# Seven block products instead of eight in eight chunks of each up-projection, on one Trainium2 core

## The chip, the cores and the metric

The kernel runs on one core of one Trainium2 chip. The metric is the device time of one execution in microseconds, 1455.82 us in the median of three runs before the change (1455.78 to 1455.86). The engines of the core are TensorE (PE in the profile, its weight loads PEld), VectorE (DVE), ScalarE (ACT), GpSimd (POOL) and SyncE (SP); all work in their own order and wait for each other on semaphores. SP and POOL issue the transfers here.

## The reference, cut to what matters

Two layers on a sequence of 512 tokens with 1024 features: attention and a gated FFN, then a recurrent block and a gated FFN. What the change touches is the first half of the FFN:

```python
def conv_ffn(x, w_up, conv_w, conv_b, w_down):
    u = causal_dwconv(x @ w_up, conv_w, conv_b)      # w_up: 1024 x 6144, conv over 3 tokens
    g, v = u[..., :D_FF], u[..., D_FF:]              # D_FF = 3072
    return (jax.nn.gelu(g, approximate=True) * v) @ w_down
```

All is float32.

## The kernel before

**Precision.** Each float32 operand is split into two float32r tiles, a rounded one (hi) and the rest (lo). `split` (line 148) is an ACT copy for hi and a DVE subtraction for lo. A product is three matmuls, hi by hi, hi by lo and lo by hi (`PASSES`, `mm3`, line 257).

**The up-projection.** Features lie on partitions and tokens in the free dimension. A weight chunk is 256 columns of w_up, a load of 1 MB that SP issues (`load`, line 193). It makes two units of 128 columns, hi and lo. A tile is one unit against the transposed activations hT: 8 blocks of 128 features, three passes, 24 matmuls with 512 tokens each, into one PSUM bank (`feat`). For each of 12 values of j, `ffn` (line 591) runs four tiles: two Gelu tiles (chunk j of the g half) and two value tiles (chunk j of the v half). Only the first j is made in token halves, as matmuls 256 tokens wide. After each tile `sink` (line 607) evacuates it: `conv` (line 594) is an ACT pass with scale and bias (L596) and two DVE multiply-adds that read the bank shifted by one and two tokens (L600); a Gelu tile gets an ACT Gelu (L611), a value tile a DVE product with the Gelu tile (L615). The 24 product tiles stay in SBUF for the down-projection (`rows_run`).

**What sets the order.** The schedule is written by hand: the order in the code is the order on each engine. After each tile `tick` (line 222) advances pending side work (norms) and calls `pump` (line 167), which splits the next weight units as long as fewer than 8 (`W_UNITS`) are live, and issues loads into three raw buffers. `take` (line 209) returns a unit, `done` (line 216) frees it. So weights are split up to 8 tiles ahead, and a split waits on ACT until PE has left its buffer.

**Other buffers.** The residual x lies in `x_sb`, written in `postnorm` (L411) and read in `prenorm`. The general pool `gen` has 32 tiles of 128x512, the norm gains have two tiles of 128x1024, and PSUM has 8 banks in rotation.

Of the kernel before, what the change touches and what calls it, by code (L numbers as in the profile page):

```python
# [18 lines left out]
P = 128  # L19
# [13 lines left out]
W_UNITS = 8  # L33
# [4 lines left out]
WARM = 5  # L38

# [35 lines left out]
def kernel(  # L75
# [30 lines left out]
    wp = ctx.enter_context(tc.tile_pool(name="wp", bufs=W_UNITS))  # L106
# [24 lines left out]
    x_sb = cp.tile([P, 4, D], F32, tag="x_sb", name="x_sb")  # L131
# [21 lines left out]
    state = {"dma": 0, "cv": 0, "live": 0, "next": 0, "hold": False}  # L153
# [12 lines left out]

    def pump(limit=2):

        for _ in range(limit):
            i = state["cv"]  # L170
            if not pieces and i < state["dma"]:
                pieces.extend((i, j, u) for j, u in enumerate(parts_of(plan[i][0], raws.pop(i))))
                state["cv"] += 1
            if pieces and state["live"] < W_UNITS:
                i, j, raw = pieces.pop(0)
                hi, lo = (
                    wp.tile([P] + list(raw.shape[1:]), F32R, tag=t, name=nm("w" + t)) for t in ("hi", "lo")
                )
                h = raw.shape[1] // 2
                cuts = [(slice(None), slice(0, h)), (slice(None), slice(h, 2 * h))]  # L180
                if raw.shape[1] == 1:
                    cuts = [(slice(None), slice(0, 1), slice(n, n + 512)) for n in (0, 512)]
                if plan[i][4] is not None:
                    split_normed(hi, lo, raw, plan[i][4] + (2 * j if plan[i][0] == "value" else 0))
                    cuts = []
                for c in cuts:
                    split(hi[c], lo[c], raw[c])
                units[i, j] = (hi, lo)
                state["live"] += 1
            while not pieces and state["dma"] < len(plan) and state["dma"] - state["cv"] < RAW_BUFS:  # L190
                load()
# [17 lines left out]
    def take(i, j):  # L209
        while (i, j) not in units:  # L210
            before = state["live"]
            pump(1)
            assert before != state["live"]
        return units[i, j]

    def done(n=1):
        state["live"] -= n
# [19 lines left out]
    def w_cols(w, c0, normed=False):  # L237
# [4 lines left out]
        plan.append(("feat", KD, 256, srcs, 0 if normed else None))  # L242
# [72 lines left out]
    def prenorm(t, hT, g, wait):  # L315
        xh, gh = halves(x_sb[:, t, :]), halves(g)
# [31 lines left out]
    def first_transposed(t, i):  # L348

        ps = psum("tr")  # L350
        for k in range(4 * i, 4 * i + 4):
            nc.tensor.transpose(
                ps[:, k % 4 * P : (k % 4 + 1) * P],
                x_sb[:, t, i * 512 : i * 512 + 512].rearrange("t (p k) -> t k p", k=4)[:, k % 4], ident,
            )
# [16 lines left out]
    def first_squares(i):  # L372
        for t in range(4):
            junk = gen(s="junk")
            nc.scalar.activation(
                junk, x_sb[:, t, i * 512 : i * 512 + 512], AF.Square, accum_out=first_ss[i][:, t : t + 1]
# [23 lines left out]
    def postnorm(t, banks, g, final):  # L400
# [8 lines left out]
        for i, c in enumerate(at):  # L409
            xc = x_sb[:, t, c]  # L410
# [12 lines left out]
    def feat(W, hT, dst, n0, n1):  # L423
        for k in range(KD):
            mm3(
                dst[:, n0:n1],
                [w[:, k, :] for w in W],
# [5 lines left out]
    def feat_tiles(n, hT, sink, halves=False):  # L433
# [15 lines left out]
        for c in range(n):  # L449
            i = chunk()  # L450
            for m in range(2):
                ps = psum()
                feat(take(i, m), hT, ps, 0, S)
                done()
                sink(2 * c + m, ps)
                tick()
# [18 lines left out]
    def rows_run(nchunks, A, prep, seq, order, post, pre, eng):  # L475
# [7 lines left out]
        def product(t, i, k, cols, start, stop):  # L483
            w = take(*W[k // 2][k % 2])
            c0 = i * 512
# [3 lines left out]
                [v[:, 0, c0 + cols.start : c0 + cols.stop] for v in w],  # L489
# [101 lines left out]
    def ffn(layer, hT, post, pre):  # L591
# [14 lines left out]

        def sink(b, ps, j):
            m = b % 2
            if b < 2:
                u = conv(ps, 2 * j + m)  # L610
                nc.scalar.activation(u, u, AF.Gelu_apprx_tanh)  # L611
                gv.append(u)
            else:
                u = conv(ps, 24 + 2 * j + m)
                nc.vector.tensor_tensor(gv[2 * j + m], gv[2 * j + m], u, op=ALU.mult)  # L615
# [4 lines left out]
        for j in range(12):  # L620
            if j == 11:
                prep(3)
            feat_tiles(2, hT, lambda b, ps: sink(b, ps, j), j == 0)
        return run()


    def attention(hT, post, pre):
# [50 lines left out]
        def first_values(vs):  # L678
# [4 lines left out]
            def product(t, u, which=range(6)):  # L683
                W = take(ids[u // 2], u % 2)
                steps = [(k, a, b) for a, b in PASSES for k in (2 * u, 2 * u + 1)]
                for n in which:
# [4 lines left out]
                        W[b][:, k % 2, :],  # L691
# [24 lines left out]
            done(2)  # L716
# [12 lines left out]
            done(2)  # L729
# [15 lines left out]
        def values(vs, permute, midway=None):  # L745
# [6 lines left out]
            for t in range(4):  # L752
                banks[t] = psum("v")
                for u in range(4):
                    W = take(ids[u // 2], u % 2)
                    steps = [(k, a, b) for k in (2 * u, 2 * u + 1) for a, b in PASSES]
                    for k, a, b in steps:
# [3 lines left out]
                            W[b][:, k % 2, :],  # L761
# [3 lines left out]
                    if t == 3 and u % 2:  # L765
                        done(2)
# [190 lines left out]
    def lru(hT, post, pre):  # L957
# [19 lines left out]
        def gates(n):  # L977
            W = take(chunk(), 0)
            sg = {}
            for m in range(2):  # L980
                for gx in range(2):
                    ps = psum("gate")
                    for k in range(2):
                        mm3(ps, [w[:, 2 * gx + k, m * P : (m + 1) * P] for w in W], xs[2 * n + k], k == 0, k == 1)
# [79 lines left out]
    for layer in range(2):  # L1064
# [9 lines left out]
        for j in range(12):  # L1074
            w_cols(ffn_w_up[layer], j * 256)
            w_cols(ffn_w_up[layer], D_FF + j * 256)
# [12 lines left out]
    def x_half(t, i):  # L1089
        c = slice(i * 512, (i + 1) * 512)  # L1090
        nc.sync.dma_start(x_sb[:, t, c], x[0, t * P : (t + 1) * P, c])
# [72 lines left out]
```

## Time and profile before

| What | before |
|---|---|
| median of 3 runs | 1455.82 us |
| span of the profiled execution, first to last instruction | 1454.0 us |
| what lies around the span, against the median | 1.8 us |
| mean granted TensorE clock | 0.999 |
| VectorE (DVE) busy | 879.8 us, 61% |
| ScalarE (ACT) busy | 675.9 us, 46% |
| GpSimd (POOL) busy | 133.9 us, 9% |
| moved by DMA | 172.76 MB, mean 119 GB/s |

The profile is of one execution. Its span leaves out what comes before the first and after the last instruction; the execution's own time isn't printed beside it, so 1.8 us, the median less the span, stands for that. A matmul's row is longer than the time by which the next follows it, since matmuls are pipelined; the spacing of the start times is what a matmul costs. The stretch of the chunks that change (j = 3 to 10) runs from 568.3 to 742.4 us in the first layer and from 1121 to 1295 us in the second.

### The profile page before, as it was taken

To read this page: it belongs to the slowest core of one execution; us is meant where nothing else is said; L and a number is where in the kernel's file an instruction comes from. 1 tells how busy PE (TensorE), PEld (TensorE's weight loads), DVE (VectorE), ACT (ScalarE), POOL (GpSimd) and SP (SyncE) were. 2 spreads that over 40 slices of the span, in tenths; PEclk is the share of its full clock that TensorE was granted. 3 is DMA by queue.
4 is the path that set the end of the run, shared out by engine and by line. 5 is a ranking of instruction groups with operands and counts; after the bars stand their busy time and mean duration, and the time that the engine had idled before them with its cause. 6 is when DMAs were issued, how large, how long until landed. Compare 5 with 4: busy or idle time off the path is not lost.

```text
span 1454.0 us, 18793 instructions
## 1 busy us (share of the span) xinstructions
PE 1445.0 (99%) x6861; PEld 1214.4 (84%) x6861; DVE 879.8 (61%) x1955; ACT 675.9 (46%) x1532; POOL 133.9 (9%) x275
## 2 busy tenths in 40 slices
PE   9999999999999999999999999999999999999998
PEld 7888888888888898888888888888898888888886
DVE  6767747474735975555564338769775555564333
ACT  7656636262615553343444335589453434444221
POOL 0340414040402100000000001000100000000000
PEclk9999999999999999999999999999999999999999
DMA  7653637372726343323323322432333233223201
GB/s 225 207 146 109 174 113 208 104 215 97 216 96 211 102 131 100 103 87 102 101 88 116 115 73 88 131 116 84 120 102 116 87 102 102 87 104 128 88 0 58
DMA packets 125364, 172.76 MB, mean 119 GB/s; under 512 B 8736, under 2 KB 102392, under 8 KB 125272
## 3 DMA queue, kind: packets, MB, share of 16 engines
q1 hardware_dynamic: 114280, 145.48, 31.0%
q0 software_dynamic: 10144, 25.04, 5.9%
q8 instruction: 54, 0.88, 0.2%
q10 hardware_dynamic: 848, 1.05, 0.2%
q14 instruction: 38, 0.31, 0.1%
HBM read 156.24 MB, written 15.29 MB: 118 GB/s over the span
## 4 chain that ended last, share of the span: by engine, by line
PE 93%; ACT 4%; DVE 3%; issue 1%; DVEq 0%; ACTq 0%
PE ps L259 55%; PE acc L259 24%; PE v L758 8%; PE v L688 1%; DVE xb L967 1%; PE O L909 1%; PE S L854 1%; PE S L808 1%; DVE wlo L150 1%; ACT sig L988 1%; ACT whi L149 1%; PE O L259 1%; PE tr L341 1%; ACT sig L1007 0%; ACT a L1005 0%
## 5 line engine op out<-in xcount | busy, mean ns | idle before, releaser
L259 PE MATMUL ps<-hT,whi 128*128 128x512 f32 (+1 forms) x2752 | 801.3, 375 | 0.0
L259 PEld LDWEIGHTS ps<-hT,whi 128*128 128x128 f32 x2752 | 503.6, 188 | 91.6
L259 PE MATMUL ps<-hT,wlo 128*128 128x512 f32 (+1 forms) x1376 | 515.3, 374 | 0.0
L150 DVE TENSOR_TENSOR wlo<-raw,whi 128x512 fp32r<-128x512 f32 x360 | 230.8, 686 | 187.2 <-ACT whi L149 187.1
L259 PEld LDWEIGHTS ps<-hT,wlo 128*128 128x128 f32 x1376 | 259.1, 188 | 46.5
L149 ACT ACTIVATE whi<-raw 128x512 fp32r<-128x512 f32 x360 | 204.6, 621 | 135.4 <-PE acc L259 121.0
L600 DVE SCALAR_TENSOR_TENSOR u<-ps,cols,u 128x511 f32<-128x511 f32 x192 | 143.8, 749 | 140.6 <-ACT u L596 137.2
L259 PE MATMUL acc<-whi,ahi 128*128 128x512 f32 x512 | 199.7, 390 | 0.0
L259 PE MATMUL acc<-whi,alo 128*128 128x512 f32 x512 | 199.4, 389 | 0.1
L259 PE MATMUL acc<-wlo,ahi 128*128 128x512 f32 x512 | 199.3, 389 | 0.0
L143 ACT ACTIVATE whi<-raw,first_w 128x128 fp32r<-128x128 f32 (+1 forms) x432 | 146.2, 425 | 56.6 <-PE ps L259 33.9
L596 ACT ACTIVATE u<-ps,cols 128x512 f32<-128x512 f32 x96 | 74.8, 779 | 210.0 <-PE ps L259 210.0
L144 DVE SCALAR_TENSOR_TENSOR wlo<-raw,first_w,whi 128x128 fp32r<-128x128 f32 (+1 forms) x432 | 139.5, 389 | 1.4 <-ACT whi L143 1.3
L259 PEld LDWEIGHTS acc<-whi,alo 128*128 128x128 f32 x512 | 96.1, 188 | 20.5 <-DVE alo L150 0.5
L259 PEld LDWEIGHTS acc<-whi,ahi 128*128 128x128 f32 x512 | 96.1, 188 | 19.8
L259 PEld LDWEIGHTS acc<-wlo,ahi 128*128 128x128 f32 x512 | 96.2, 188 | 19.8
L758 PE MATMUL v<-whi,hT 128*128 128x512 f32 x320 | 102.4, 393 | 0.0
L302 POOL DMA_DIRECT2D turned<-T x36 | 19.6, 547 | 763.4 <-DVE T L296 759.9
L309 POOL DMA_DIRECT2D ft<-turned x144 | 78.7, 554 | 39.6 <-issue 17.7
L758 PEld LDWEIGHTS v<-whi,hT 128*128 128x128 f32 x320 | 60.1, 188 | 12.3
L611 ACT ACTIVATE u<-u 128x512 f32<-128x512 f32 x48 | 30.3, 632 | 80.4 <-DVE u L600 80.4
L758 PE MATMUL v<-wlo,hT 128*128 128x512 f32 x160 | 62.3, 389 | 0.0
(171 smaller groups left out, 1010.7 us busy)
## 6 DMA issues: line engine op xcount, KB each, us to landing
raw<-in_ffn_w_up_dram SPq DMA_DIRECT2D x48, 1024.0 KB
raw<-in_attn_w_qkv_dram SPq DMA_DIRECT2D x67, 512.0 KB
raw<-in_ffn_w_down_dram SPq DMA_DIRECT2D x24, 1024.0 KB
raw<-in_lru_w_in_dram SPq DMA_DIRECT2D x8, 1024.0 KB
turned<-T POOLq DMA_DIRECT2D x28, 256.0 KB, 2.6
ft<-turned POOLq DMA_DIRECT2D x112, 64.0 KB, 5.8
vrows<-v SPq DMA_DIRECT2D x16, 256.0 KB
vp<-vrows SPq DMA_DIRECT2D x16, 256.0 KB
```

Source lines behind the costliest of these rows:

```text
L143: nc.scalar.activation(hi[:, k], raw[:, k], AF.Copy, scale=w)
L144: nc.vector.scalar_tensor_tensor(lo[:, k], raw[:, k], w, hi[:, k].bitcast(F32), op0=ALU.mult, op1=ALU.subtract)
L149: nc.scalar.activation(hi, raw, AF.Copy)
L150: nc.vector.tensor_tensor(lo, raw, hi.bitcast(F32), op=ALU.subtract)
L259: mm(dst, l[a], r[b], start=start and n == 0, stop=stop and n == 2)
L302: nc.gpsimd.dma_start(d, T)
L309: nc.gpsimd.dma_start(t[32 * c : 32 * c + 32].rearrange("j (b x) -> j b x", b=4), d.rearrange("(b j) (c x) -> c j b x", j=32, c=4)[c],)
L341: nc.tensor.transpose(ps[:, k * P : (k + 1) * P], xs[i][:, k * P : (k + 1) * P], ident)
L596: nc.scalar.activation(u, ps, AF.Identity, scale=cc[:, j : j + 1], bias=cc[:, 48 + j : 49 + j])
L600: nc.vector.scalar_tensor_tensor(u[:, d:], ps[:, : S - d], wc, u[:, d:], op0=ALU.mult, op1=ALU.add)
L611: nc.scalar.activation(u, u, AF.Gelu_apprx_tanh)
L758: mm(banks[t], hT[a][:, k, t * P : (t + 1) * P], W[b][:, k % 2, :], start=(k, a, b) == (0, 0, 0), stop=(k, a, b) == (KD - 1, 1, 0),)
```

## The change

In chunks j = 3 to 10 of both FFNs the two Gelu tiles are no longer made one after the other. Weights and activations of the pair are cut in 2 x 2 blocks: the 1024 features of the sum into halves, the 256 outputs into two tiles, the 512 tokens into halves. The product of the two 2 x 2 matrices is made by Strassen's scheme (Winograd's form) from seven block products instead of eight. Each block product is 4 blocks of features by three passes, 12 matmuls 256 tokens wide. Value tiles and all other chunks stay as they were.

- **Weight sums.** Each changed chunk gives seven half units (`HALF`): four blocks and sums of blocks. They are made in place in the raw tile: two by accumulating DMAs that POOL issues (`add_rows`: the block of w_up is read a second time and added), two by DVE additions (`across`, `upper`). Each half unit is split into hi and lo.
- **Token sums.** Four sums of blocks of hT are made once per layer by side steps during j = 1 and 2 (`token_sums`): 8 POOL additions (hi + lo), 8 DVE additions and subtractions, 8 splits. Their tiles take the place of `x_sb` (stored to DRAM before, fetched after by `x_back`), of the two gain tiles and of four `gen` tiles.
- **The order.** A round of 15 slots has the seven products of one pair and eight quarters of value tiles (6 matmuls of 512 each). A pair's products stand in slots 0 (product 5), 3 (1), 4 (3), 8 (2), 9 (6), 14 (7) and 20 (4, in the next round); quarters stand in 1, 2, 6, 7 and 10 to 13. The partial results are combined in two PSUM banks per pair: ACT copies product 5 out (after slot 1), and after slot 5 copies the half bank c to z and minus the half bank a into c; DVE writes z - c after slot 10 and c - p5 after slot 15. PE goes on accumulating on what ACT wrote.
- **Evacuation.** `conv` as before; the Gelu or the product follows two slots later (`begin`, `finish`).
- **Units.** The pool has 16 half units of 4 blocks in place of 8 units of 8 blocks, the same bytes. `tick` runs after each slot.

The diff, cut to its core:

```diff
-W_UNITS = 8
+HALVES = 16
+SEVEN = range(3, 11)
+AT = {5: 0, 1: 3, 3: 4, 2: 8, 6: 9, 7: 14, 4: 20}
+CYCLE = 15
...
+    def add_rows(to, src):
+        nc.gpsimd.dma_start(to, src, accum_op=ALU.add)
+
+    def ahead(i):
+        add_rows(blocks(i)["s1"], plan[i][3][0][0][:, 4:8, P:256])
...
+            def across(i=i):
+                x = blocks(i)
+                nc.vector.tensor_tensor(x["s1"], x["s1"], x["w11"], op=ALU.add)
+
+            def upper(i=i):
+                x = blocks(i)
+                nc.vector.tensor_tensor(x["w12"], x["w12"], x["s1"], op=ALU.add)
+                add_rows(x["w11"], plan[i][3][0][0][:, 0:4, P:256])
...
+            for at, item in (
+                (-6, (None, lambda i=i: ahead(i))), (0, ("s1", "s1")), (0.1, (None, across)), (1, ("w12", "w12")),
+                (2, ("w11", "w11")), (2.1, (None, upper)), (4, ("s4", "w12")), (5, ("s2", "s1")), (6, value(0)),
+                (8, ("a22", "a22")), (10, ("s3", "w11")), (11, value(1)),
+            ):
...
-            pump(1 if state["live"] >= W_UNITS - 2 else 2)
+            pump(1 if state["live"] >= HALVES - 4 else 2)
...
-        for j in range(12):
-            if j == 11:
-                prep(3)
-            feat_tiles(2, hT, lambda b, ps: sink(b, ps, j), j == 0)
+        for j in range(SEVEN[0]):
+            if j == 1:
+                side(token_sums(hT, T))
...
+        i = seven(hT, T, begin, i)
+        x_back()
+        prep(3)
...
+    def token_sums(hT, T):
+        d = dp.tile([P, 4, D], F32, name=nm("x_kept"))
+        nc.gpsimd.dma_start(d, X[0])
...
+            nc.gpsimd.tensor_tensor(o, hi.bitcast(F32), lo.bitcast(F32), op=ALU.add)
...
+            def step(n):
+                name, b = LEFT[n]
+                W = take(i, name)
...
+                for k in range(4):
+                    for q, (wa, ha) in enumerate(PASSES):
+                        mm(
+                            y[b][:, 0:256], W[wa][0][:, k, :], right[n](ha, k), start=n in (1, 5) and k == q == 0,
+                            stop=k == 3 and q == 2, skip_group_check=True,
+                        )
+                done(1)
+                if n == 5:
+                    later(1, lambda: nc.scalar.activation(p5, c, AF.Copy))
+                elif n == 3:
+                    def seed():
+                        nc.scalar.activation(z, c, AF.Copy)
+                        nc.scalar.activation(c, a, AF.Copy, scale=-1.0)
+                    later(1, seed)
+                elif n == 6:
+                    later(1, lambda: nc.vector.tensor_tensor(y[0][:, 256:512], z, c, op=ALU.subtract))
+                    later(2, lambda: finish(b0, y[0], j))
+                elif n == 7:
+                    later(1, lambda: nc.vector.tensor_tensor(y[1][:, 256:512], c, p5, op=ALU.subtract))
+                elif n == 4:
+                    later(1, lambda: finish(b0 + 1, y[1], j))
```

`later(n, f)` emits f after the n-th slot from now.

More of the change, by code (lines that the diff above doesn't have):

```diff
@@ new lines, in refill @@
+    def refill():
+        i = state["cv"]
+        if i >= state["dma"]:
+            return
+        if plan[i][0] == "seven":
+            n = 1
+            while plan[i + 2 * n][0] == "seven":
+                n += 1
+            pieces.extend(stream(i, n))
+            state["cv"] += 2 * n
+        else:
+            if plan[i + 1 : i + 2] and plan[i + 1][0] == "seven":
+                pieces.append((None, lambda: ahead(i + 1)))
+            parts = parts_of(plan[i][0], raws[i])
+            pieces.extend(plain(i, j, r, j == len(parts) - 1) for j, r in enumerate(parts))
+            state["cv"] += 1
@@ L167, in pump @@
     def pump(limit=2):
         for _ in range(limit):
[L170 to L189, printed above, removed]
@@ L191, in pump @@
+            while state["dma"] < len(plan) and state["dma"] - state["used"] < RAW_BUFS:
                 load()
@@ L488, in product @@
                 [a[:, t * P : (t + 1) * P] for a in A[k]],
[L489 removed]
+                [v[i][:, 0, cols] for v in w],
                 start,
@@ L1074 @@
         for j in range(12):
-            w_cols(ffn_w_up[layer], j * 256)
-            w_cols(ffn_w_up[layer], D_FF + j * 256)
+            for half in range(2):
+                w_cols(ffn_w_up[layer], half * D_FF + j * 256, kind="seven" if j in SEVEN and not half else "feat")
         for c in range(12):
```

246 lines of the change are left out of this document (212 added, 34 removed).

## The prediction

> **What bounds the kernel now.** I read the page first: the engines' busy shares and the chain of work that ended last.
>
> ```profile
> span 1454.0 us, 18793 instructions
> ...
> PE 1445.0 (99%) x6861; PEld 1214.4 (84%) x6861; DVE 879.8 (61%) x1955; ACT 675.9 (46%) x1532; POOL 133.9 (9%) x275
> ...
> PE 93%; ACT 4%; DVE 3%; issue 1%; DVEq 0%; ACTq 0%
> ```
>
> PE is the chain, nearly everywhere. Then the chain over the up-projection of the first layer alone: its last piece is one run of matmuls from 510.50 us to the end of the window.
>
> ```profile
> 510.50 249.69 PE ps L259 x1158
> ```
>
> Then the stretches of both layers in which the changed chunks lie (columns: window, its length, busy time of PE, PEld, DVE, ACT and POOL with their instructions, granted clock, DMA share, GB/s).
>
> ```profile
> 568.30:742.40 174.10, 174.10 (x770) 144.22 (x769) 98.98 (x144) 68.41 (x112) 0.00 (x0) 1.00 0.29 97
> 1121.00:1295.00 174.00, 174.00 (x769) 144.15 (x768) 98.97 (x144) 68.35 (x112) 0.00 (x0) 1.00 0.30 97
> 1050.00:1077.00 27.00, 27.00 (x219) 26.57 (x218) 21.35 (x53) 14.87 (x32) 0.56 (x1) 1.00 0.24 74
> ```
>
> PE has no gap in them; DVE works 57% of the time, ACT 39%, POOL not at all, at full clock. So here time is what PE needs, and removed matmuls are removed time as long as the others keep up. The third row holds the token halves of j = 0 in the second layer: with 256-wide matmuls the weight loads are busy 26.57 of 27 us, which matters below.
>
> **Price of a matmul.** A matmul costs the spacing of starts. PE's timeline where the first layer goes from 512 to 256 wide, and back (start, length, what, count):
>
> ```profile
> 499.74 0.39 PE L259 MATMUL acc<-whi,alo 128*128 128x512 f32 x1
> 499.97 0.40 PE L259 MATMUL ps<-hT,whi 128*128 128x256 f32 x2
> ...
> 500.32 0.40 PE L259 MATMUL ps<-hT,whi 128*128 128x256 f32 x2
> ...
> 515.00 0.40 PE L259 MATMUL ps<-hT,whi 128*128 128x256 f32 x2
> ...
> 524.36 0.40 PE L259 MATMUL ps<-hT,whi 128*128 128x256 f32 x2
> ...
> 524.72 0.63 PE L259 MATMUL ps<-hT,whi 128*128 128x512 f32 x2
> ...
> 525.42 0.62 PE L259 MATMUL ps<-hT,whi 128*128 128x512 f32 x2
> ...
> 526.11 0.61 PE L259 MATMUL ps<-hT,whi 128*128 128x512 f32 x2
> ...
> 530.19 0.61 PE L259 MATMUL ps<-hT,whi 128*128 128x512 f32 x2
> ```
>
> Rows come in triples (two hi, one lo). From 515.00 to 524.36 are 26 triples, 78 matmuls in 9.36 us: **0.1200 us** at 256 wide. From 526.11 to 530.19 are 6 triples, 18 in 4.08: **0.2267 us** at 512. Half the width costs 53%, not 50%: the two spacings differ by 0.1067 for 256 tokens, so 0.0133 us is fixed per matmul. More matmuls, each narrower, eat part of Strassen's eighth.
>
> The Trainium skill ("TensorE: Matmul & The Clock Gate", Back-to-back issue gap) gives 81 ns per matmul at N=128 and 131 ns at N=512 as the sustained roofline of weight load and matmul. On a straight line that is some 98 ns at 256, an estimate from that page: 84 x 98 = 8.2 against 48 x 131 = 6.3 us, and the change would lose 1.9 us a pair. Its isolated gap, N/2.4 + 2.5 ns, would gain 48 x 215.8 - 84 x 109.2 ns = 1.2 us. The rows above agree with the slope of the latter, with a fixed part of 13 ns; they decide.
>
> **The change, part by part.**
>
> *Products.* A pair of Gelu tiles was 2 x 24 matmuls: 48 x 0.2267 = 10.88 us. Seven products are 7 x 12 = 84 matmuls: 84 x 0.1200 = 10.08 us. Gain 0.80 us a pair; 8 chunks in 2 layers are 16 pairs: **-12.8 us**.
>
> *Switches of width.* The first triple after a switch to 512 took 0.70 us (524.72 to 525.42) where a settled one takes 0.68; the first after a switch to 256 took 0.35 (499.97 to 500.32) where 0.36 is usual. A round of 15 slots has three switches each way: 3 x 16 x (0.02 - 0.01) = **+0.5 us**.
>
> *Work of DVE and ACT in a round.* Groups in the first stretch (line, engine, operation, count | busy, mean ns | idle before it and for what):
>
> ```profile
> L150 DVE TENSOR_TENSOR wlo<-raw,whi 128x512 fp32r<-128x512 f32 x64 | 41.3, 686 | 20.5 <-ACT whi L149 20.5
> L149 ACT ACTIVATE whi<-raw 128x512 fp32r<-128x512 f32 x64 | 36.5, 618 | 0.0
> L596 ACT ACTIVATE u<-ps,cols 128x512 f32<-128x512 f32 x32 | 25.0, 781 | 79.1 <-PE ps L259 79.1
> L600 DVE SCALAR_TENSOR_TENSOR u<-ps,cols,u 128x511 f32<-128x511 f32 x32 | 24.0, 750 | 52.9 <-ACT u L596 52.9
> L611 ACT ACTIVATE u<-u 128x512 f32<-128x512 f32 x16 | 10.1, 632 | 26.6 <-DVE u L600 26.6
> ```
>
> Before, per j: 98.98/8 = 12.37 us of DVE and 68.41/8 = 8.55 of ACT in 21.76. Added: 3 splits (11 half units for 8), 2 weight additions of the split's shape, 2 half-width subtractions on DVE and 3 half-width copies on ACT. Half-width rows exist only in SBUF, in the attention:
>
> ```profile
> L830 ACT ACTIVATE phi<-ft x16: 402/518/633, 75.3 to 191.3; 128x512 fp32r<-128x512 f32 x8, 128x256 fp32r<-128x256 f32 x8
> L831 DVE TENSOR_TENSOR plo<-ft,phi x16: 416/553/693, 79.3 to 192.1; 128x512 fp32r<-128x512 f32 x8, 128x256 fp32r<-128x256 f32 x8
> ```
>
> So a PSUM copy lies between 0.40 (half width, SBUF) and 0.78 (L596, full width, PSUM), a subtraction between 0.42 and 0.75; I take 0.45, near the half-width rows. DVE: 12.37 + 5 x 0.686 + 2 x 0.45 = 16.7 us; ACT: 8.55 + 3 x 0.618 + 3 x 0.45 = 11.8 us, in a round of 10.08 + 8 x 1.36 = 20.96. That is 80% and 56%; with the upper ends 17.3 and 12.7. Neither becomes the bound: cost **0** while queues don't bunch.
>
> *The added waits.* PE now waits inside a pair, and behind a waiting matmul stands all PE work. Product 5's copy is emitted after slot 1, and product 3 in slot 4 needs it: from the end of product 5 that leaves slots 1, 2, 3, so 2 x 1.36 + 1.44 = 4.16 us for 0.45 us of work. The two copies after product 3 have slots 5, 6, 7: also 4.16 us, for 0.9. z - c has slots 10 to 13, 5.44 us, for 0.45; c - p5 has 7.0 us. ACT and DVE take their queues in order, so ahead of such an operation may stand a split, a conv pass and a Gelu (0.62 + 0.78 + 0.63 = 2.0 us on ACT), or conv and product on DVE (2.2 us). Both fit. Weights are split up to 16 half units ahead, one and a half rounds. Cost **0**; as the upper bound both of ACT's limits are missed by a whole such queue, 2 x 2.0 = 4 us a round.
>
> *Accumulating DMAs.* No row shows one. Near rows are plain POOL transfers: 256 KB of long rows, and the 64 KB pieces of 512-byte rows of ft, whose landing took 2.0 to 8.8 us.
>
> ```profile
> turned<-T POOLq DMA_DIRECT2D x28, 256.0 KB, 2.6
> ...
> gain<-in_norm_ffn_post_dram POOLq DMA_DIRECT2D x2, 512.0 KB, 4.0
> ```
>
> ```profile
> DMA to landing us min/median/max: 2.0/5.6/8.8
> ```
>
> An addition is 256 KB in 512-byte rows and must read its destination too, so I bound it by 2.6 below and twice 8.8 = 17.6 above, and take twice 2.6, some 5 us, nearest to the row of its size. The second addition of a chunk (into w11) is issued a split and an addition (some 2 us) after slot 15 of the round and read by a split after slot 23: four quarters and four products, 5.44 + 5.76 = 11.2 us, so 9.2 from its issue. If it is late, ACT stops at that split with conv and copies behind it, and DVE with it; z - c then is due before product 7, 6.9 us later, and needs 0.62 + 0.69 + 0.69 + 0.45 = 2.5 of them. So PE waits only when the landing takes over 9.2 + 4.4 = **13.6 us**. The first addition has more. Taken: **0**.
>
> *Token sums.* In the seven tiles before the first chain:
>
> ```profile
> 530.20:568.30 38.10, 38.10 (x170) 31.56 (x169) 24.15 (x36) 15.17 (x25) 0.00 (x0) 1.00 0.34 111
> ```
>
> To DVE's 24.15 us come 16 operations of 0.686 = 11.0 and two or three weight additions, 2: 37 of 38 us. The third, fourth and fifth tile carry most of it. DVE's spacing in a run is shorter than its rows, 527.98 to 528.59 = 0.61 us, and conv is 1.56:
>
> ```profile
> 526.42 1.53 DVE L600 SCALAR_TENSOR_TENSOR u<-ps,cols,u 128x511 f32<-128x511 f32 x2
> 527.98 0.69 DVE L615 TENSOR_TENSOR u<-u,u 128x512 f32<-128x512 f32 x1
> 528.59 1.29 DVE L150 TENSOR_TENSOR wlo<-raw,whi 128x512 fp32r<-128x512 f32 x2
> ```
>
> With these the three tiles' queues are 6.4, 7.0 and 5.8 us against 5.44 of PE: DVE falls 2.9 us behind, and the two tiles after them (3.4 and 4.6) give 2.9 back. ACT, which waits for conv before each Gelu, reaches product 5's copy close to its limit. POOL's eight additions have no row; the nearest is an operation on 128 columns,
>
> ```profile
> masks.py:199 POOL TENSOR_SCALAR_AFFINE_SELECT ident<-ident 128x128 f32<-128x128 f32 x1 | 0.3, 287 | 0.1
> ```
>
> four of which are 1.15 us, so 9 us for eight, and double that if DVE's reads get in their way; the first is used two tiles (10.9 us) later. The store of x to DRAM (2 MB; by the row of 512 KB some 16 us) is issued two tiles ahead of the first sum's split and goes beside splits made 8 tiles ahead; the fetch after the chains, and the gains' loads behind it in POOL's queue, are read first by norms after the down-projection's first nine chunks. The additions read 0.5 MB more per 2 MB, which lifts the DMA share from 0.29 to some 0.37; SP's loads stay in number and wait for the same three buffers. I take **+1.0 us a layer, 2 in all**, bounds 0 and 4 a layer.
>
> *Sum.* -12.8 + 0.5 + 2.0 = -10.3. The execution's span of 1454.0 becomes 1443.7; the median of the runs shown stands 1.8 above that span, so **1445.5 us**.
>
> **The rivals.**
>
> *Small waits in every round.* DVE at 80% is late now and then, ACT's Gelu waits for it, and the copies between products come after their 4.16 us. For it: before, every Gelu already waits for conv (26.6 us over 16 in L611's row). Against: 2.0 us of queue in 4.16. At 0.35 us a round, 16 rounds lose 5.6: 1451. From 0.64 us a round, 10.3/16, the gain is gone: 1456. The upper bound, 4 us a round, would be 1455.8 - 10.3 + 64 = 1510.
>
> *The accumulating DMA is late (ends on the other side).* Each us of landing beyond 13.6 costs 16 us; from 14.2 on the change is slower. At the upper bound of 17.6 it is 4 x 16 = 64: 1445.5 + 64 = 1510. For it: 512-byte rows, descriptors that POOL makes, and no row of an addition. Against: those pieces landed within 8.8 us though several were under way together, and the row of 256 KB stands at 2.6.
>
> *The narrow products run at the pace of weight loads.* Each matmul has its own load, 188 ns long by its row, and PEld was 98% busy in the 256-wide stretch. If fresh weights every 12 matmuls kept loads from overlapping, a pair would take 84 x 0.188 = 15.8 us, +4.9: 1455.8 + 16 x 4.9 = 1534; slower from 10.88/84 = 0.1295 us a matmul.
>
> ```profile
> L259 PEld LDWEIGHTS ps<-hT,whi 128*128 128x128 f32 x2752 | 503.6, 188 | 91.6
> ```
>
> Against: token halves also load for each matmul, at 0.1200. The 81 and 131 ns of the Trainium skill (same page and section) point this way; the spacings shown do not.
>
> **How the numbers follow.** The forecast, with all waits covered, has 0.66, from 1442.5 (no stall at all, 1443.0, less 0.5) to 1448.5 (entry 3 us worse). Small waits have 0.18: 0.12 with a gain left (1448.5 to 1452.9), 0.06 with none to tell. The late addition has 0.13, the weight loads 0.03. A measurement of this kernel tells about 0.2%, 2.9 us. So faster 0.66 + 0.12 = 0.78, same 0.06, slower 0.16. The range that holds eight in ten runs from 1442.5 to 1453.5, nearly all the cases but the slower ones.
>
> **What would show it.** Right: in the stretches of the chains PE without idle time, products of 1.44 us at 0.120 spacing, each round 21 us, DVE near 80%, POOL's additions landing in about 5 us. Wrong: PE waiting for ACT's copies at products 3, 2 and 6 or for DVE at 7 and 4 (the first rival); ACT's split waiting for a DMA into raw, landing over 13 us (the second); a spacing over 0.13 in the chains (the third); a wait only at the first chain of each layer (the token sums mis-sized).

## The result and the profile after

The changed kernel takes **1470.53 us** (median of 4 runs, 1470.17 to 1470.63) against 1455.82 for the kernel before on the same chip (three runs of 1455.78 to 1455.86; a fourth took 2971.36 us and is left out): ratio 1.010, interval 1.0085 to 1.0115. It is 14.7 us slower where 10.3 faster was forecast, and lies far above the range. The profiled execution took 1470.55 us.

In the changed kernel L340 holds the wide matmuls, L830 those of the seven products, L153 and L154 the split (ACT copy, DVE subtraction), L683 conv, L695 and L697 Gelu and value product, L749 the token additions, L836 the copy of product 5, L841 the seed that product 2 waits for.

The page of the changed kernel, the lines that answer to those of before (fourth: the largest group of narrow products that read hT; last: the accumulating DMAs, count, size, median from issue to landing):

```profile
span 1468.7 us, 20562 instructions
...
PE 1438.2 (98%) x7437; PEld 1233.6 (84%) x7437; DVE 983.2 (67%) x2099; ACT 735.2 (50%) x1644; POOL 197.6 (13%) x327
...
PE 83%; DVE 10%; ACT 5%; issue 1%; DMA 0%; DVEq 0%; ACTq 0%
...
L830 PE MATMUL ps<-hT,whi 128*128 128x256 f32 x384 | 72.9, 289 | 21.9 <-ACT part L836 20.8
...
raw<-in_ffn_w_up_dram POOLq DMA_DIRECT2D x32, 256.0 KB, 4.7
```

PE is busy for 6.8 us less than before, in a span that is 14.7 longer. The chain of work has handed 10% to DVE, from 3%. One wait stands out in the groups: narrow products waited 20.8 us for ACT's copy at L836, product 5's copy to SBUF.

The same kernel by windows (columns as in the prediction): the stretch of the token sums up to the wait, the wait, the time right after it, and the two rounds that follow.

```profile
530.20:568.30 38.10, 38.10 (x179) 31.92 (x178) 34.93 (x38) 11.01 (x19) 12.98 (x11) 1.00 0.47 131
568.90:579.20 10.30, 0.06 (x1) 0.00 (x0) 8.84 (x15) 8.38 (x17) 0.00 (x0) 0.75 0.08 23
579.20:584.20 5.00, 4.96 (x18) 4.48 (x19) 4.33 (x8) 1.10 (x3) 0.94 (x1) 0.50 0.97 327
589.63:610.57 20.94, 20.94 (x134) 18.99 (x133) 15.40 (x25) 11.59 (x20) 2.58 (x2) 1.00 0.53 128
610.57:631.50 20.93, 20.93 (x133) 18.98 (x133) 16.15 (x26) 11.48 (x20) 2.58 (x2) 1.00 0.52 127
```

The rounds are what was forecast: 20.93 us each (forecast 20.96) against 21.76, PE without a gap, DVE 16.15 us (77%). Eight rounds gain 8 x 0.83 = 6.6 us a layer. Nearly all that is lost is lost once a layer, at product 3 of the first chain, which needs product 5's copy: 10.3 us in which PE stands, then 5 us at half clock. The waits of PE, sum, times and longest, say that it is this place in both layers and almost no other (the longest of the rest, 1.5 us, stands in the kernel before too):

```profile
PE ps L830 <- ACT part L836: 20.8, 2, 10.5
PE ps L830 <- ACT ps L841: 1.1, 2, 0.6
```

Going back from the wait. PE's timeline where the first chain waits, with the rows that price the half clock:

```profile
568.68 0.28 PE L830 MATMUL ps<-hT,wlo 128*128 128x256 f32 x1
579.24 0.80 PE L830 MATMUL ps<-hT,whi 128*128 128x256 f32 x2 [10.28 <-ACT part L836]
...
581.96 1.05 PE L340 MATMUL ps<-hT,whi 128*128 128x512 f32 x2
...
584.41 0.63 PE L340 MATMUL ps<-hT,whi 128*128 128x512 f32 x2
...
586.52 0.50 PE L830 MATMUL ps<-hT,whi 128*128 128x256 f32 x2 [0.55 <-ACT ps L841]
```

The 12 narrow matmuls from 579.24 to 581.96 took 2.72 us where 1.44 is usual, the next 6 wide ones to 584.41 took 2.45 where 1.36 is: 2.4 us for the clock. ACT's queue shows why the copy was late: its Gelu had waited 14.45 us for DVE's conv (first row). From there on ACT stays late: it waits again for DVE's token sums (second row), and four splits stand ahead of the copy (the last row):

```profile
546.01 0.63 ACT L695 ACTIVATE u<-u 128x512 f32<-128x512 f32 x1 [14.45 <-DVE u L683]
...
562.73 0.64 ACT L153 ACTIVATE T<-B 128x512 fp32r<-128x512 f32 x1 [4.36 <-DVE B L771]
...
576.74 2.17 ACT L153 ACTIVATE whi<-raw 128x512 fp32r<-128x512 f32 x4
578.82 0.36 ACT L836 ACTIVATE part<-ps 128x256 f32<-128x256 f32 x1
```

And DVE, whose conv came so late, beside POOL:

```profile
528.98 12.12 DVE L154 TENSOR_TENSOR wlo<-raw,whi 128x512 fp32r<-128x512 f32 x2
541.02 1.52 DVE L683 SCALAR_TENSOR_TENSOR u<-ps,cols,u 128x511 f32<-128x511 f32 x2
```

```profile
528.64 1.33 POOL L191 DMA_DIRECT2D raw<-in_ffn_w_up_dram  x1 [37.78 <-DVE u L683]
529.44 1.10 POOL L736 DMA_DIRECT2D x_kept<-x_sb  x1
530.02 10.52 POOL L749 TENSOR_TENSOR B<-hT,hT 128x512 f32<-128x512 f32 x8
```

Two of DVE's subtractions, 1.29 us in the kernel before, took 12.12; the first was as long as ever, and all of the rest fell on the second. They end 0.6 us after POOL's eight token additions, which ran through in 10.52 us. POOL's additions were off every path by the working of the prediction; here the engine beside them stood still until they were done, and everything that DVE feeds stood with it.

The account of one layer: +10.3 wait, +0.6 second wait (L841, the seed), +2.4 half clock, -6.6 rounds: +6.7. Two layers make 13.4 of the 14.7. Taken by the starts of the matmuls, the losses are 13.5 us in the first layer and 13.8 in the second, not 13.3, and PE's work on the first up-projection began 0.4 us later (510.64 against 510.25 us); the last 0.3 us is open.

### The profile page after: what moved, and what is told of

Same layout as the page of the kernel before. It is cut to its first block, busy times and chain, and to the rows that moved or that the text cites. A ratio compares the mean times of both kernels' runs of the same rounds, so it can differ in the third digit from the quotient of the medians.

```text
span 1468.7 us, 20562 instructions
## 1 busy us (share of the span) xinstructions
PE 1438.2 (98%) x7437; PEld 1233.6 (84%) x7437; DVE 983.2 (67%) x2099; ACT 735.2 (50%) x1644; POOL 197.6 (13%) x327
## 4 chain that ended last, share of the span: by engine, by line
PE 83%; DVE 10%; ACT 5%; issue 1%; DMA 0%; DVEq 0%; ACTq 0%
PE ps L340 36%; PE acc L340 24%; PE ps L830 10%; PE v L1024 7%; DVE wlo L154 4%; DVE u L683 2%; PE v L954 2%; DVE xb L1233 1%; ACT whi L153 1%; PE O L1175 1%; PE S L1120 1%; PE S L1074 1%; ACT sig L1254 1%; PE O L340 1%; PE tr L422 1%
## 5 line engine op out<-in xcount | busy, mean ns | idle before, releaser
L340 PE MATMUL ps<-hT,whi 128*128 128x512 f32 (+1 forms) x2240 | 646.7, 374 | 0.0
L340 PEld LDWEIGHTS ps<-hT,whi 128*128 128x128 f32 x2240 | 405.0, 189 | 68.9
L154 DVE TENSOR_TENSOR wlo<-raw,whi 128x512 fp32r<-128x512 f32 x408 | 291.1, 741 | 191.3 <-ACT whi L153 191.3
L340 PE MATMUL ps<-hT,wlo 128*128 128x512 f32 (+1 forms) x1120 | 416.4, 372 | 0.0
L153 ACT ACTIVATE whi<-raw 128x512 fp32r<-128x512 f32 x408 | 244.4, 626 | 227.1 <-PE acc L340 118.2
L340 PEld LDWEIGHTS ps<-hT,wlo 128*128 128x128 f32 x1120 | 211.6, 189 | 37.3
L340 PE MATMUL acc<-whi,ahi 128*128 128x512 f32 x512 | 199.6, 390 | 0.0
L340 PE MATMUL acc<-whi,alo 128*128 128x512 f32 x512 | 199.3, 389 | 0.1
L340 PE MATMUL acc<-wlo,ahi 128*128 128x512 f32 x512 | 199.2, 389 | 0.0
L683 DVE SCALAR_TENSOR_TENSOR u<-ps,cols,u 128x511 f32<-128x511 f32 x192 | 143.6, 748 | 42.6 <-ACT u L679 39.2
L340 PEld LDWEIGHTS acc<-whi,alo 128*128 128x128 f32 x512 | 96.1, 188 | 20.3 <-DVE alo L154 0.5
L340 PEld LDWEIGHTS acc<-whi,ahi 128*128 128x128 f32 x512 | 96.1, 188 | 19.9
L340 PEld LDWEIGHTS acc<-wlo,ahi 128*128 128x128 f32 x512 | 96.1, 188 | 19.9
L830 PE MATMUL ps<-hT,whi 128*128 128x256 f32 x384 | 72.9, 289 | 21.9 <-ACT part L836 20.8
L830 PE MATMUL ps<-T,whi 128*128 128x256 f32 x512 | 92.8, 280 | 0.0
L191 POOL DMA_DIRECT2D raw<-in_ffn_w_up_dram x32 | 41.5, 1471 | 369.5 <-DVE wlo L154 211.8
L830 PEld LDWEIGHTS ps<-hT,whi 128*128 128x128 f32 x384 | 63.5, 197 | 25.5 <-ACT part L836 21.2
```

Source lines behind the costliest of these rows:

```text
L153: nc.scalar.activation(hi, raw, AF.Copy)
L154: nc.vector.tensor_tensor(lo, raw, hi.bitcast(F32), op=ALU.subtract)
L191: nc.gpsimd.dma_start(to, src, accum_op=ALU.add)
L340: mm(dst, l[a], r[b], start=start and n == 0, stop=stop and n == 2)
L683: nc.vector.scalar_tensor_tensor(u[:, d:], ps[:, : S - d], wc, u[:, d:], op0=ALU.mult, op1=ALU.add)
L830: mm(y[b][:, 0:256], W[wa][0][:, k, :], right[n](ha, k), start=n in (1, 5) and k == q == 0, stop=k == 3 and q == 2, skip_group_check=True,)
```

## Experiments

Two theories at first. **Lock:** POOL's additions keep DVE out, and DVE's 11 lost us arrive at PE. **Overload:** the sums are too much work for DVE and ACT in seven tiles, whoever adds, and the long row is only how a busy stretch looks. A third candidate was the 2 MB store in front of the additions.

### The eight additions on DVE

```diff
-            nc.gpsimd.tensor_tensor(o, hi.bitcast(F32), lo.bitcast(F32), op=ALU.add)
+            nc.vector.tensor_tensor(o, hi.bitcast(F32), lo.bitcast(F32), op=ALU.add)
```

> The eight additions hi + lo of each layer's token sums on DVE instead of POOL, nothing else. Lock theory (while POOL's eight additions run, 10.5 us, a DVE operation with two SBUF inputs stands still, and this is what makes PE wait at the first product 3): DVE pays 8 x 0.61 = 4.9 us instead of 10.7, so PE's wait of 10.3 us a layer falls to some 4 to 5 us and the time to 1455 to 1459. Overload theory (the sums are simply too much DVE work ahead of the first chain, whoever adds): 4.9 us more on DVE, the wait grows to 15 us, 1479 to 1482. Store theory (the 2 MB store of x beside it holds DVE): a DVE row of 12 us is still there and the time does not fall.

Measured: 1455.61 us, ratio to before 1.000 (0.9991 to 1.001), 14.9 us less than the changed kernel. DVE's row of the additions, and PE's waits:

```profile
538.94 4.89 DVE L749 TENSOR_TENSOR B<-hT,hT 128x512 f32<-128x512 f32 x8
```

```profile
PE ps L830 <- ACT part L836: 5.8, 2, 2.9
PE ps L830 <- ACT ps L841: 2.7, 2, 1.4
```

What the lock cost DVE 11 us for costs 4.89 when DVE does it itself. More work on DVE is less time: the overload theory falls as the main cause. It keeps the rest: 2.9 + 1.4 = 4.3 us a layer of waits remain in the first chain, and the time is still 12 us over the 1443.5 that the prediction had without its token sums.

### Copies by ACT in place of the additions

Here the lo part is left out of the token sums, so that neither DVE nor POOL adds; the store stays.

```diff
-            nc.gpsimd.tensor_tensor(o, hi.bitcast(F32), lo.bitcast(F32), op=ALU.add)
+            nc.scalar.activation(o, hi.bitcast(F32), AF.Copy)
```

> The eight additions are replaced by eight ACT copies of hi; the lo parts of the activations are left out of the token sums. Lock theory: no POOL addition, no DVE row over 2 us, PE's wait at the first product 3 is 0 to 2 us a layer, 1443 to 1448. Overload theory: DVE's own work is unchanged and ACT has 5 us more, so the wait stays near 10 us, about 1470. Store theory: DVE's row of 12 us stays, about 1470.

Measured: 1457.03 us, ratio 1.001 (1.0001 to 1.0019): a miss by 9 us. ACT's row, and DVE's next subtraction behind it:

```profile
539.69 4.26 ACT L749 ACTIVATE B<-hT 128x512 f32<-128x512 f32 x8
```

```profile
544.51 0.69 DVE L154 TENSOR_TENSOR wlo<-raw,whi 128x512 fp32r<-128x512 f32 x1 [5.45 <-ACT whi L153]
```

No DVE row is stretched though the store runs as before: between the issue and the landing of POOL's transfers no subtraction is longer than 0.69 us. So the store by itself does not stop DVE. But eight operations in one bunch in front of ACT's splits cost as much as a bunch on DVE: PE waits 3.6 and up to 2.8 us a layer. The stretch ahead of product 3 has no room for a bunch of 4 to 5 us on either engine.

### From chunk 4 on, with the additions on POOL and on DVE

```diff
-SEVEN = range(3, 11)
+SEVEN = range(4, 11)
```

alone, then with the edit of the first experiment as well. Seven chunks a layer instead of eight, and four more tiles between the sums and the first chain.

> Block products only in chunks 4 to 10 (seven pairs a layer); the token sums, on POOL, stay where they are, so there are four more tiles (21.8 us) between them and the first chain. Lock theory and overload theory both: DVE is still locked for some 10.7 us, but has four tiles with 43% of idle time to come back, so PE does not wait; 14 pairs at 0.83 us are 11.6 us: 1443.5 to 1446. If chains lose time in themselves, by a theory that the steady rounds are not what they seem, the time stays above 1456.

> Block products only in chunks 4 to 10, and the eight additions on DVE. In the run from chunk 4 with POOL's additions they had started in the norms of the first chunk, since POOL does not wait for PE, and PE waited there for a transpose's input. Lock theory: without POOL's additions this wait of 1.6 us a layer and what follows it (PE's run began 2.1 us late) is gone and nothing replaces it, since DVE has four more tiles for its 4.9 us: 1450.4 - 2 x 2.1 = 1446. Overload theory: 4.9 us more on DVE, no better than 1450.

Measured: 1450.43 us (0.9963, 0.9948 to 0.9977) with POOL, **1446.52 us** (0.9936, 0.9921 to 0.9951) with DVE. The second came as expected; one wait is left in it:

```profile
PE ps L830 <- ACT ps L841: 1.3, 2, 0.6
```

The first missed by over 4 us: nothing in POOL's queue held its work back any more, and it started in the norms ahead of the FFN, where PE's transposes waited 3.3 us for DVE in the two layers. POOL, and DVE beside it:

```profile
507.05 0.56 POOL L736 DMA_DIRECT2D x_kept<-x_sb  x1 [15.93 <-PE tr L422]
507.62 2.54 POOL L749 TENSOR_TENSOR B<-hT,hT 128x512 f32<-128x512 f32 x2
514.10 9.82 POOL L749 TENSOR_TENSOR B<-hT,hT 128x512 f32<-128x512 f32 x6 [3.94 <-DVE hT L427]
```

```profile
507.52 3.20 DVE L401 TENSOR_TENSOR xs<-x_sb,gain 128x512 f32<-128x512 f32 x1
...
514.54 9.93 DVE L154 TENSOR_TENSOR wlo<-raw,whi 128x512 fp32r<-128x512 f32 x6
```

The first pair cost DVE 3.20 - 0.68 = 2.5 us, the whole pair. Beside the six, DVE's six subtractions took 9.93 instead of some 3.7: 1.0 us more each, which is turn by turn. Both patterns stand in one kernel, and the difference was not yet understood.

### The kernel before with eight additions that nobody reads

Added work only: eight POOL additions of hT, issued before chunk 4's tiles; then, in a second kernel, of product tiles, which hold them back to chunk 5.

```diff
+            if j == 4:
+                dead = [gen(s="B") for _ in range(8)]
+                for n in range(8):
...
+                    nc.gpsimd.tensor_tensor(o, hi.bitcast(F32), lo.bitcast(F32), op=ALU.add)
             feat_tiles(2, hT, lambda b, ps: sink(b, ps, j), j == 0)
```

```diff
+            if j == 5:
+                for _ in range(8):
+                    nc.gpsimd.tensor_tensor(gen(s="B"), gv[8], gv[9], op=ALU.add)
             feat_tiles(2, hT, lambda b, ps: sink(b, ps, j), j == 0)
```

> The kernel before, with eight POOL additions (hi + lo of the activations into eight general tiles that nobody reads) put ahead of chunk 4 of each up-projection; no store of x, no sums. Lock theory: one DVE operation with two SBUF inputs gets a row of 10 to 12 us beside them, DVE catches up in the idle 43% of the next tiles, PE does not wait, 1455.5 to 1456.5. Store or overload theory: no DVE row over 2 us.

> The kernel before with eight POOL additions of two 128x512 SBUF tiles in each up-projection, whose result nobody reads; they read the last Gelu products of chunk 4, so they cannot start before chunk 5. Lock theory: DVE rows with two SBUF inputs of 10 us or more beside POOL's 10.5 us; PE has units split up to 8 tiles ahead and DVE is idle 43% of the time, so PE does not wait: 1455.3 to 1456.3. If POOL and DVE only shared the port and took turns, no DVE row would be over 3 us. If the lock by itself reaches PE, 1460 and more.

Measured: 1463.76 us (1.0055, 1.0038 to 1.0072) and 1455.80 us (1.000). The first missed: with nothing to wait for, POOL ran in the norms again, four additions in 5.61 us from 500.01 on, and even DVE's operations on one column, 0.15 us elsewhere, waited:

```profile
501.89 1.25 DVE L272 SCALAR_TENSOR_TENSOR s<-s,s 128x1 f32<-128x1 f32 x1
```

The second, POOL and DVE in the steady stretch:

```profile
616.74 11.64 POOL L625 TENSOR_TENSOR B<-u,u 128x512 f32<-128x512 f32 x8 [124.81 <-issue]
```

```profile
622.50 3.47 DVE L150 TENSOR_TENSOR wlo<-raw,whi 128x512 fp32r<-128x512 f32 x2 [1.28 <-ACT whi L149]
```

This pair of DVE's subtractions lost 3.47 - 1.29 = 2.2 us, and one before it 1.1: 3.3 in all, not 11. The place decides the price (8 us where PE waits for DVE, none where DVE has slack), but the long row did not come back. Something else was in the changed kernel.

### The sums spread over the tiles, on DVE and on POOL

The first sum is split first, the second and third at the first and sixth slot of the first round, the fourth after its additions at the ninth; the additions run in pairs, each just ahead of its use. The first kernel has them on DVE, the second on POOL.

```diff
-        for n, k0 in at:
-            for k in range(2):
-                B[k, n] = both(k0 + 2 * k, n[1])
-        yield 1
+        b11 = pair(0, 0)
+        yield 1
+        b12 = pair(1, 0)
+        yield 1
...
+        yield 5
+        parted(2, b12)
+        yield 3
+        b21 = pair(0, 4)
```

> Chunks 3 to 10 as in the changed kernel. The additions are on DVE, and the token sums are spread: the first sum (needed by product 5) stays ahead of the chain, the others are made up to ten slots into the first round, each before its product. The same work in all. Lock and load theory together (the loss is only bunched DVE time ahead of the first chain: 10.7 us of lock in the changed kernel, 4.9 us of additions with DVE's): 10 DVE operations fewer ahead of product 3, so no wait over 1 us, and 16 pairs at 0.83 us: 1442.5 to 1445. A theory that the steady rounds lose as well: above 1450.

> The paced sums, but with the additions on POOL again, in pairs at four places. Lock theory: each pair locks DVE for some 2.6 us where DVE's own pair takes 1.2, so 5.6 us of DVE time a layer more than the paced kernel with DVE's additions; spread out, most is absorbed: PE waits 0 to 2 us a layer, 1443 to 1448. Burst theory (only the run of eight in a row harms): as the paced kernel with DVE's additions.

Measured: 1449.36 us on DVE (0.9953, 0.9937 to 0.997), 1458.85 on POOL (1.0018, 1.0009 to 1.0027). Both missed, by 4 and by 11 us. On DVE one wait was left, at product 2, and ACT's queue shows it:

```profile
PE ps L836 <- ACT ps L847: 3.7, 2, 1.8
```

```profile
572.09 2.19 ACT L153 ACTIVATE whi<-raw 128x512 fp32r<-128x512 f32 x4 [3.96 <-DVE raw L209]
574.19 0.36 ACT L846 ACTIVATE part<-ps 128x256 f32<-128x256 f32 x1
574.58 0.37 ACT L847 ACTIVATE ps<-ps 128x256 f32<-128x256 f32 x1
```

Four weight splits stand ahead of the seed in ACT's queue and wait 3.96 us for DVE's weight sum, which stands behind the spread sums in DVE's queue. Spreading took the first wait away and put its work into the first round. On POOL, rows of POOL and DVE from two places:

```profile
530.25 5.56 POOL L749 TENSOR_TENSOR B<-hT,hT 128x512 f32<-128x512 f32 x4
551.58 1.30 POOL L191 DMA_DIRECT2D raw<-in_ffn_w_up_dram  x1 [15.77 <-DVE wlo L154]
552.42 3.02 POOL L749 TENSOR_TENSOR B<-hT,hT 128x512 f32<-128x512 f32 x2
```

```profile
528.97 7.39 DVE L154 TENSOR_TENSOR wlo<-raw,whi 128x512 fp32r<-128x512 f32 x2
...
553.35 2.65 DVE L697 TENSOR_TENSOR u<-u,u 128x512 f32<-128x512 f32 x1
```

Four additions cost DVE 7.39 - 1.29 = 6.1 us, two cost it 2.65 - 0.69 = 2.0 (3.3 at a third place), and it resumes only when POOL's run is over. Eight cost 10.8. The loss follows the length of the run, and in each of these cases POOL had issued a DMA right ahead of it. In the kernels that took turns, it had not.

### The same spread sums from chunk 4 on

Both edits:

```diff
-SEVEN = range(3, 11)
+SEVEN = range(4, 11)
```

and the spread on DVE.

> Chunks 4 to 10 as seven products, the additions on VectorE and the token sums spread over the tiles and the first round (both edits run alone before: 1446.5 from chunk 4 with the sums in a bunch, 1449.4 from chunk 3 with the sums spread). Bunched work ahead of the first chain is the theory for what is left: from chunk 4 one wait of 0.6 us a layer remained; four more tiles for the spread sums take it away: 1445.0 to 1446.0. If the wait at product 2 belongs to the round itself (the splits ahead of the seed copies on ScalarE wait for VectorE's weight sum), it stays or grows to 1.8 us a layer: 1446.5 to 1449.

Measured: 1450.48 us (0.9965, 0.9952 to 0.9977), above both expected ranges and 4 us more than with the sums in a bunch.

```profile
PE ps L836 <- ACT ps L847: 3.7, 2, 1.8
```

The wait at product 2 is the same 1.8 us a layer with four more tiles ahead of it: it comes from what was put into the first round, not from too little time before. That explains 2 x (1.8 - 0.6) = 2.4 of the 4 us; the profiled run of this kernel, 1448.8, was at the low end of its runs, and the rest stays open.

### A transfer issued ahead of the additions

The kernel before with eight dead additions of hT at the place where the changed kernel has them, held back by a small POOL addition that reads the first product tile; then the same with the store of x, 2 MB, issued by POOL between the small addition and the eight.

```diff
+            if j == 1:
+                gate = gen(s="B")
+                nc.gpsimd.tensor_tensor(gate[:, 0:4], gv[0][:, 0:4], gv[1][:, 0:4], op=ALU.add)
+                for n in range(8):
...
+                    nc.gpsimd.tensor_tensor(o, hi.bitcast(F32), lo.bitcast(F32), op=ALU.add)
```

and for the second kernel, ahead of that loop,

```diff
+                nc.gpsimd.dma_start(dp.tile([P, 4, D], F32, name=nm("x_kept")), x_sb)
```

> The kernel before, with eight POOL additions of the two parts of hT whose results nobody reads (added work: only these), held back by a small POOL addition that reads the first product tile of j = 0, so that they start about where the changed kernel's eight stood, near 528 us, as a run without anything between them. If POOL shuts VectorE out for a whole run of such additions: one VectorE row of about 11 us at 529 (12.12 us in the changed kernel), and the time still within 0.2% of 1455.8, since VectorE has 37% of slack there and PSUM has 8 banks. If the two engines take turns, as with the additions of product tiles at chunk 5: no VectorE row over 4 us, POOL's eight take 11 to 12 us, same time; the long row of the changed kernel would then need something besides the additions (the 2 MB store in front of them).

> The kernel before with the eight dead additions of hT behind the same small gate, and now the 2 MB store of x issued by POOL between the gate and the eight (added work only). Without the store the two engines took turns: two VectorE rows of 3.2 us, POOL's eight in 11.85. If a transfer issued by POOL right ahead of the additions is what lets POOL keep VectorE out: one VectorE row of 6 to 11 us beside the eight additions, which then take 10.5 us, and the time within 0.2% of 1455.8, because nothing here needs VectorE within 10 us. If the transfer does not matter: VectorE rows of 4 us at most and 11 to 12 us for the eight.

Measured: 1455.81 us (1.0001, 0.9991 to 1.001) and 1455.82 us (1.000, 0.9991 to 1.001); neither costs time there, as DVE has slack. Without the transfer, POOL and DVE:

```profile
533.39 11.85 POOL L629 TENSOR_TENSOR B<-hT,hT 128x512 f32<-128x512 f32 x8
```

```profile
536.70 3.18 DVE L150 TENSOR_TENSOR wlo<-raw,whi 128x512 fp32r<-128x512 f32 x2 [1.28 <-ACT whi L149]
...
542.60 3.19 DVE L150 TENSOR_TENSOR wlo<-raw,whi 128x512 fp32r<-128x512 f32 x2 [1.28 <-ACT whi L149]
```

With it:

```profile
532.66 0.58 POOL L626 DMA_DIRECT2D x_kept<-x_sb  x1
533.26 10.03 POOL L630 TENSOR_TENSOR B<-hT,hT 128x512 f32<-128x512 f32 x8
```

```profile
533.16 1.52 DVE L600 SCALAR_TENSOR_TENSOR u<-ps,cols,u 128x511 f32<-128x511 f32 x2
535.96 8.48 DVE L150 TENSOR_TENSOR wlo<-raw,whi 128x512 fp32r<-128x512 f32 x2 [1.28 <-ACT whi L149]
```

One line decides. Without the transfer each pair of subtractions loses 1.9 us and POOL's eight stretch to 11.85; with it POOL runs through in 10.03 and the pair, begun 2.7 us into the run, waits until the run is over: 8.48 us. The conv at 533.16, whose one large input in SBUF goes with one in PSUM, is not touched. The second layer has the same row, 8.47 us. The store had landed before the run was over; from issue to landing, over the two layers:

```profile
DMA to landing us min/median/max: 7.3/8.0/8.7
```

In the first layer it landed at 540.0 us, in the second 8.7 us after its issue. Two more additions began after the landing in the first layer, and the subtraction stayed out to their end, 543.8 us: once begun, the lock does not need the transfer to be under way.

### A small addition between the transfer and the eight

```diff
         B = {}
+        tiny = gen(s="B")
+        nc.gpsimd.tensor_tensor(tiny[:, 0:4], hT[0][:, 0, 0:4].bitcast(F32), hT[1][:, 0, 0:4].bitcast(F32), op=ALU.add)
         for n, k0 in at:
```

> The changed kernel with one small POOL addition (128x4) put between the transfers that POOL issues and the eight additions, nothing else. If only the neighbourhood of a transfer and a large addition makes the long lock: VectorE and POOL take turns, no VectorE row over 5 us near 530, and the time falls to 1456 to 1463, between 1455.6 (additions on VectorE) and 1470.5. If the lock, once begun behind a transfer, lasts for the whole backlog of POOL's queue: the 12 us row stays, 1470 to 1471.

Measured: 1466.41 us (1.0072, 1.0057 to 1.0087). POOL, then DVE:

```profile
530.32 10.50 POOL L749 TENSOR_TENSOR B<-hT,hT 128x512 f32<-128x512 f32 x8
```

```profile
531.77 9.60 DVE L697 TENSOR_TENSOR u<-u,u 128x512 f32<-128x512 f32 x1
```

The lock stays, as the second theory had it, on another operation with two inputs in SBUF; but not its price: DVE got the second subtraction and a conv done first and lost 9.60 - 0.69 = 8.9 us, 1.9 us less a layer than in the changed kernel. The time is 4.1 us less than the changed kernel's, with up to 8.4 us of wait a layer in place of 10.5. That a start 0.3 us later is what let DVE finish these two is likely, but was not tested.

## Why the prediction was wrong, step by step

**What bounds the kernel** was right: PE's time is the time, and in the rounds it has no gap.

**Products, switches of width** were right: -12.8 + 0.5 was forecast, and 16 rounds at 20.93 instead of 21.76 us give -13.3. The narrow products held their 0.120 us; the third rival, with the two sustained figures of the Trainium skill behind it, did not happen.

**Work of DVE and ACT in a round** was right: forecast 16.7 and 11.8 us, measured 16.15 and 11.48, and no wait, so the first rival did not happen either. **The added waits** cost 0 in the rounds, as taken. **The accumulating DMAs** landed in 4.7 us (taken 5); the slower-than-before rival of a late addition did not happen.

**Token sums** is the step that failed. It was taken at +1.0 us a layer with 4 as its upper bound; it measured 10.3 + 0.6 + 2.4 = 13.3. Three things in it were wrong:

- The prediction priced POOL's additions by their own length ("9 us for eight, and double that if DVE's reads get in their way"). The length was good, 10.52 us. The direction was not: POOL got in DVE's way. That the additions were hidden was no cover, because the engine that should have hidden them was the one that stopped. This is 14.9 us of the kernel, the difference to the same additions on DVE.
- The working had DVE at 37 of 38 us in that stretch and called it covered, with a deficit of 2.9 us given back by two later tiles. Without the lock, with all additions on DVE, 4.3 us a layer of waits remained, and the time was 12.1 over the 1443.5: 6 us a layer, above the bound too (behind its wait of 2.9 us PE ran at half clock again, which cost some 1.6 us). A stretch that is full on paper loses whatever bunches in it. The deficit was reckoned for DVE alone; ACT, which stands behind DVE before every Gelu, inherited it.
- A wait of PE was priced at its length. The half clock after it comes on top: 2.4 us after 10.3.

None of the three rivals was the cause. What the prediction named as the sign of mis-sized token sums, a wait only at the first chain of each layer, is what the trace shows.

On the lock itself, the Trainium skill ("SBUF — State Buffer", SBUF: two separate sides) says that a DVE instruction with two inputs in SBUF contends with a GpSimd instruction that reads SBUF, and that the first to start holds the shared ports for its whole instruction while the other fully blocks. The runs without a transfer in front agree: a subtraction waited for about one addition (1.9 us for two). Behind a transfer the measurement goes further: DVE was out for two, four or eight instructions, the whole run. What holds the ports from one addition to the next there is not known. Neither a transfer alone nor additions alone did it, and the lock outlasted the store's landing. Whether the additions must follow the issuing of the transfer at once, or begin while it is under way, was not tried. The six additions of the chunk-4 kernel that took turns began after a wait of POOL, 0.5 us after the store had landed in the first layer and 0.5 us before it did in the second; that is a hint for the issuing, no more.

**The better version** is the one from chunk 4 with the additions on DVE: 1446.52 us, ratio 0.9936 to before. It gives up one chunk's gain (2 x 0.83 us) and leaves 0.6 us a layer of the waits.

## What to carry to other kernels

Work given to POOL is only free if DVE's operations with two SBUF inputs can stand still for the whole run of it, above all when POOL has just issued a transfer; price it as DVE time of the same length, then ask whether DVE would do it faster itself (4.9 us here, against 10.8). Before a stage that cannot wait, count the queues of every engine behind the one that is full, since "37 of 38 us" is a wait, not a cover. A change whose gain per round is right can still lose at its entrance: price the first round by itself.

## What the runs showed of the hardware that was not expected

- In a run, one POOL addition of 128x512 float32 follows the other by 1.24 to 1.25 us (eight take 10.03 to 10.52), on DVE by 0.61 (4.89 for eight). A run right behind a transfer issued by POOL keeps DVE's two-input operations out to its end; a run that follows something else lets DVE in after each addition, and then eight take 11.64 to 11.85 us.
- Operations on a single column were held too: up to 1.25 us instead of 0.15, beside POOL's additions.
- After PE had stood for 10.3 us, the granted clock was 0.50 for 5.0 us, in both layers, though PE was busy throughout. The Trainium skill ("TensorE: Matmul & The Clock Gate", Part 1) gives some 3.4 us of work before full speed returns; here it was 5. A wait of 2.9 us (first layer, the additions on DVE) was enough to bring the half clock back: the granted clock was 0.51 over 2.0 us, and 12 narrow matmuls took 2.72 us again, where 1.44 is usual.
- An accumulating DMA of 256 KB in 512-byte rows lands in 4.7 us, against 2.6 for a plain one of that size in longer rows.
